# Eleven small stores of the first chunk, issued from ScalarE's queue instead of SyncE's

## The chip, the core and the metric

The kernel runs on one core of a Trainium2 chip. The core has compute engines that work side by side (here VectorE, ScalarE and a little GpSimd are used), a SyncE that does no arithmetic and issues transfers, and 16 DMA engines that move data between the memory of the chip (HBM) and the core's own memory (SBUF, 128 partitions). A transfer is issued on a queue that belongs to the issuing engine; SyncE and ScalarE have one each, GpSimd has one that is filled by software. The metric is the device time of one execution in microseconds; less is better.

## What is computed

The input `logits` has the shape (2, 8, 2112, 2112) in fp32, 285 MB; the output has the same shape. A bias that depends on the distance of row and column is added, then a softmax is taken along the last axis:

```python
pos = np.arange(S)                                   # S = 2112
rel_clipped = np.clip(pos[:, None] - pos[None, :], -16, 16) + 16
logits = logits + rel_bias[:, rel_clipped][None]     # rel_bias: (8, 33)
logits = logits - logits.max(axis=-1, keepdims=True)
exp = np.exp(logits)
return exp / exp.sum(axis=-1, keepdims=True)
```

Every element is read once and written once.

## The kernel before

The 33,792 rows of the input are dealt to the 128 partitions: each holds `ROWS` = 264 rows that lie next to each other in HBM. They are worked through in `N` = 44 chunks of `R` = 6 rows per partition, 128 x 12,672 elements each (6336 KB), in `NBUF` = 4 buffers `X0` to `X3`. `STEP` = 24 rows are one round of all four buffers.

*A chunk's way.* SyncE loads it (`load`, L99). VectorE adds the bias row by row and takes the row's maximum (`add`, L238). ScalarE takes EXP of the row and its sum (`exps`, L247). VectorE then inverts three sums at a time (L255) and multiplies the three rows (L259, `scale`), raising the semaphore `scaled` by one per row. SyncE waits for six scaled rows and stores the chunk (`store`, L104). Ahead of the first chunk VectorE builds a table of the bias, for which ScalarE loads `rel_bias` (L122); GpSimd meanwhile prepares row numbers for its own late stores.

*What sets the order.* Each engine runs its instructions in the order of the code and waits on semaphores that the others raise; nothing is planned by a scheduler. SyncE first issues the loads of chunks 0 to 3 one behind the other (L129). Then it waits for chunk 0 (L285) and stores it in two portions. Rows 2 to 5 go as one transfer of 128 partitions (L286). Rows 0 and 1 go as eleven transfers (`parts`, L274 to L283): the list `AHEAD` says at which partition each begins and how many it takes, 15, 13, 4, 16, 16, 16, 9, 7, 14, 10 and 8, always every fourth partition. Each of the k partitions of such a transfer is given to another DMA engine, the first k of the 16. So one DMA engine gets from 3 to 11 of the 128 pieces of 16,896 bytes, where a transfer of all 128 partitions gives 8 to each. Near the end two other lists, `BEHIND` (SyncE, four transfers of 16) and `LAST` (GpSimd), share out rows 3 to 5 of chunk 41 (L296, L297, L159) in the opposite way.

All twelve transfers of chunk 0 raise the semaphore `main`. GpSimd waits until all twelve have landed (L169) and then raises `st[0]` in their name (L170). In the loop (L288 to L292) SyncE by turns stores the next chunk and, once the store before it has landed (`st[b]`), loads a new chunk into the buffer that has become free. The first reload, of `X0`, thus waits for the eleven small transfers too.

ScalarE's part is one loop of eleven rounds of four chunks (L268 to L270).

## Time and profile before

| | |
|---|---|
| time, median of 3 runs (lowest to highest) | 1331.28 us (1330.13 to 1331.38) |
| time of the profiled execution | 1331.03 us |
| its span, from the first to the last instruction | 1329.3 us |
| HBM read, written | 285.49 MB, 288.31 MB |
| SyncE's longest kind of wait (semaphores, L96) | 1251.0 us in 85 waits |
| loads of a chunk, issue to landing (median of 44) | 44.6 us |
| stores of a chunk, issue to landing (median of 41) | 52.6 us |

The page gives busy times for the span and for 40 equal slices of 33.2 us each; each digit is a busy share in tenths. A row of the timeline has a start, a duration, an engine (with a "q" for its instruction queue, as in SPq, where DMAs are issued), a line, an operation, and in brackets the idle time ahead of it and what ended that. The stretch view counts a packet's bytes and time in the stretch where it starts, so over a few microseconds the rate swings and a share may exceed 1. Issuing a DMA is short; moving its data comes later, when the queue has reached it.

### The profile page before, as it was taken

Reading aid. Unit: us, or ns where it says so; the run is one execution under the profiler, and the core shown is the slowest. Engines: PE = TensorE matmul, PEld = TensorE weight load, DVE = VectorE, ACT = ScalarE, POOL = GpSimd, SP = SyncE. Lnnn points to the kernel's source line nnn. Section 1 sums busy time; section 2 is a strip of 40 time slices with the busy share of each in tenths; the row PEclk is TensorE's granted clock in tenths of the full one; section 3 lists DMA queues with packets and bytes.
Section 4 is the critical chain, followed back from the end, with each engine's and each line's share of the span. In section 5 each row is a group of like instructions: output and inputs, shape, how many; then the busy total and the mean of one; then the engine's idle time right before and its main releaser. Section 6 shows DMA issues by size and latency. Waiting matters only on the chain. (4 is left out here: it accounts for less than half of the span.)

```text
span 1329.3 us, 2545 instructions
## 1 busy us (share of the span) xinstructions
DVE 977.7 (74%) x917; ACT 575.2 (43%) x539; POOL 10.0 (1%) x41
## 2 busy tenths in 40 slices
DVE  7997777677877786677778777677877786677763
ACT  3474433434444443334445433434444443334442
POOL 1000000000000000000000000000000000000100
DMA  9999999999999999999999999999999999999998
GB/s 413 414 387 427 435 435 433 435 433 435 432 436 433 433 433 433 436 435 433 432 436 433 432 435 433 435 435 435 435 432 435 432 433 435 435 435 433 433 434 356
DMA packets 13492, 571.01 MB, mean 430 GB/s; under 512 B 1824, under 2 KB 1840, under 8 KB 1840
## 3 DMA queue, kind: packets, MB, share of 16 engines
q1 hardware_dynamic: 13200, 569.33, 99.4%
q0 software_dynamic: 256, 1.62, 0.3%
q14 instruction: 4, 0.03, 0.0%
q10 hardware_dynamic: 32, 0.02, 0.0%
HBM read 285.49 MB, written 288.31 MB: 432 GB/s over the span
## 5 line engine op out<-in xcount | busy, mean ns | idle before, releaser
L238 DVE CUSTOM_DVE_ANT_0 X<-X,F 128x2112 f32<-128x2112 f32 x264 | 605.2, 2354 | 308.9 <-DVEq L96 308.9
L247 ACT ACTIVATE X<-X,nmax 128x2112 f32<-128x2112 f32 x264 | 541.7, 2052 | 539.3 <-ACTq L96 517.5
L259 DVE TENSOR_SCALAR X<-X,rec 128x2112 f32<-128x2112 f32 x264 | 332.4, 1315 | 13.2
L247 ACT ACT_TABLE_LOAD x11 | 14.1, 1283 | 188.6 <-ACTq L96 188.6
L247 ACT ACTIVATION_READ_ACCUMULATOR X<-X,nmax 128x1 f32 x264 | 49.2, 186 | 0.0
L232 DVE COPY F<-M 128x2135 f32 x11 | 26.1, 2374 | 0.5 <-DVEq L261 0.5
L238 DVE DVE_READ_ACCUMULATOR2_ANT nmax<- 128x1 f32 x264 | 21.7, 82 | 0.0
L255 DVE RECIPROCAL rec<-tot 128x3 f32<-128x3 f32 x88 | 14.9, 170 | 0.0
L159 POOL DMA_INDIRECT out_dram<-X,sel x5 | 4.5, 897 | 1239.3 <-POOLq L96 1238.1
L194 DVE TENSOR_TENSOR F<-F 128x264 f32<-128x264 f32 x1 | 0.4, 433 | 7.1 <-DMA F<-in_rel_bias_dram 7.1
L150 POOL TENSOR_SCALAR_AFFINE_SELECT sel<-sel 128x1 int32<-128x1 int32 x25 | 4.7, 190 | 3.6 <-POOL sel L144 0.2
L224 DVE COPY M<-F 128x1848 f32<-128x1848 f32 x1 | 2.1, 2077 | 0.0
L119 DVE MEMSET F<- 128x264 f32 x1 | 0.3, 278 | 1.1 <-SPq L79 1.1
L144 POOL IOTA sel<- 128x1 int32 x5 | 0.6, 127 | 0.0
L198 DVE TENSOR_REDUCE F<-F 128x33 f32<-128x264 f32 x1 | 0.6, 608 | 0.0
L221 DVE TENSOR_TENSOR M<-F 128x264 f32<-128x264 f32 x1 | 0.4, 441 | 0.0
L213 DVE TENSOR_TENSOR F<-F,rbS 128x264 f32<-128x264 f32 x1 | 0.4, 426 | 0.0
L191 DVE TENSOR_SCALAR F<-F 128x8 f32<-128x8 f32 x4 | 0.4, 165 | 0.0
L226 DVE COPY M<-rbS 128x247 f32<-128x247 f32 x1 | 0.4, 406 | 0.0
L206 DVE STREAM_TRANSPOSE F<-F 128x64 f32<-128x64 f32 x1 | 0.2, 246 | 0.0
L201 DVE STREAM_TRANSPOSE F<-F 128x64 f32<-128x64 f32 x1 | 0.2, 245 | 0.0
L211 DVE TENSOR_SCALAR F<-F,rbS 128x8 f32<-128x8 f32 x1 | 0.2, 231 | 0.0
(18 smaller groups left out, 2.8 us busy)
## 6 DMA issues: line engine op xcount, KB each, us to landing
X<-in_logits_dram SPq DMA_DIRECT2D x44, 6336.0 KB, 44.6
out_dram<-X SPq DMA_DIRECT2D x41, 6336.0 KB, 52.6
out_dram<-X SPq DMA_DIRECT2D x3, 3168.0 KB, 19.1
out_dram<-X SPq DMA_DIRECT2D x1, 4224.0 KB
out_dram<-X SPq DMA_DIRECT2D x4, 396.0 KB, 45.6
out_dram<-X SPq DMA_DIRECT2D x3, 264.0 KB
out_dram<-X SPq DMA_DIRECT2D x1, 247.5 KB
out_dram<-X SPq DMA_DIRECT2D x1, 231.0 KB
```

Of the source, the lines that this page charges most:

```text
L144: step(g.iota(col, pattern=[[0, 1]], base=(p0 * ROWS + row) // unit, channel_multiplier=lap * ROWS // unit))
L150: step(g.affine_select(out=col, in_=col, pattern=[[0, 1]], base=base, channel_multiplier=mul, compare_op=op, fill=float(FAR)))
L159: g.indirect_dma_start(out=blocks, out_offset=bass.IndirectOffsetOnAxis(ap=sel[0:n, w : w + 1], axis=0), in_=bass.AP(tensor=x.tensor, offs ...
L191: then(v.tensor_scalar(out=m, in0=dp, scalar1=0.0, scalar2=None, op0=op))
L194: then(v.tensor_tensor(out=view(F, 0, [[W, H], [1, W]]), in0=view(F, 0, [[W, H], [1, W]]), in1=view(F, SC + 3 * PB, [[1, H], [0, W]]), op= ...
L198: then(v.tensor_reduce(out=F[:, RB : RB + W], in_=view(F, 0, [[1, W], [W, H]]), axis=mybir.AxisListType.X, op=ALU.add))
L224: then(v.tensor_copy(out=view(M, U + W, [[ROWS, PB], [1, ROWS - W]]), in_=view(F, SC + 7 * PB, [[1, PB], [0, ROWS - W]])))
L232: v.tensor_copy(out=F[:, :], in_=M[:, bass.ds(ROWS - STEP - j, FW)]).then_inc(dve, 1)
L238: v.tensor_tensor_reduce(out=x, in0=x, in1=F[:, STEP - 1 - r : STEP - 1 - r + S], scale=-1.0, scalar=BIG, op0=ALU.add, op1=ALU.min, accum_ ...
L247: nc.scalar.activation(out=x, in_=x, func=EXP, scale=-1.0, bias=nmax[:, r : r + 1], accum_out=tot[:, r : r + 1],).then_inc(expd, 1)
L255: v.reciprocal(out=rec[:, r0 : r0 + HALF], in_=tot[:, r0 : r0 + HALF]).then_inc(inv, 1)
L259: v.tensor_scalar_mul(out=x, in0=x, scalar1=rec[:, r : r + 1]).then_inc(scaled, 1)
```

## The change

A new semaphore `half` is added. `parts` gets the issuing engine as a parameter. ScalarE's first round is taken out of the loop and written out; between its first chunk's six EXPs and those of the second, ScalarE waits for `half` and issues the eleven transfers `AHEAD` on its own queue. SyncE raises `half` when three rows of chunk 0 are scaled (the two that are stored are among them), and no longer issues the eleven.

```diff
+        half = nc.alloc_semaphore("half")
...
-        with nc.Fori(0, ROWS // STEP, 1, engines=[ENG.Activation]):
-            for b in range(NBUF):
-                exps(b)
-        def parts(own, x, r0, r1, j, sem):
+        def parts(eng, own, x, r0, r1, j, sem):
             step_p = list(x.ap[0])[0]
             for p, k in own:
-                nc.sync.dma_start(
+                eng.dma_start(
...
+        for b in range(NBUF):
+            exps(b)
+            if b == 0:
+                take(nc.scalar, half, 1)
+                parts(nc.scalar, AHEAD, X[0], A0, A1, 0, main)
+        with nc.Fori(1, ROWS // STEP, 1, engines=[ENG.Activation]):
+            for b in range(NBUF):
+                exps(b)
+
+        nc.sync.wait_ge(scaled, HALF)
+        nc.sync.sem_inc(half, 1)
         take(nc.sync, scaled, R)
         nc.sync.dma_start(out=rows(out, A1, R - A1), in_=X[0][:, A1 * S : R * S]).then_inc(main, 16)
-        parts(AHEAD, X[0], A0, A1, 0, main)
...
-        parts(BEHIND, late, Z0, Z1, (N - 3) * R, st[(N - 3) % NBUF])
+        parts(nc.sync, BEHIND, late, Z0, Z1, (N - 3) * R, st[(N - 3) % NBUF])
```

In the lists of instructions that follow, `X_58` to `X_61` are the buffers X0 to X3, `out_dram` is the output, and a shape is partitions x elements. Line numbers are each kernel's own; L278 of before is L273 of the change, L100 is L101, L104 is L105.

SyncE before, from the last initial load to the first reload:

```order
L100 DMA X_61<-in_logits_dram 128x12672
L119 UNCONDITIONAL_BRANCH
L286 DMA out_dram<-X_58 128x8448
L278 DMA out_dram<-X_58 15x4224
L278 DMA out_dram<-X_58 13x4224
L278 DMA out_dram<-X_58 4x4224
L278 DMA out_dram<-X_58 16x4224 x3
L278 DMA out_dram<-X_58 9x4224
L278 DMA out_dram<-X_58 7x4224
L278 DMA out_dram<-X_58 14x4224
L278 DMA out_dram<-X_58 10x4224
L278 DMA out_dram<-X_58 8x4224
```

SyncE in the change, the same place and on to the first reload:

```order
L101 DMA X_61<-in_logits_dram 128x12672
L120 UNCONDITIONAL_BRANCH
L292 DMA out_dram<-X_58 128x8448
L293 UNCONDITIONAL_BRANCH
L105 ISA
L105 DMA out_dram<-X_59 128x12672
L101 ISA
L101 DMA X_58<-in_logits_dram 128x12672
```

Behind the four-row store the eleven rows are gone; the store of the second chunk is next.

ScalarE in the change, from the table load of its first EXP to the second chunk (before, its one loop has the four rows of EXPs and nothing between them):

```order
L248 ACT_TABLE_LOAD
L248 ACTIVATE X_58,tot<-X_58,nmax 128x2112 x6
L273 DMA out_dram<-X_58 15x4224
L273 DMA out_dram<-X_58 13x4224
L273 DMA out_dram<-X_58 4x4224
L273 DMA out_dram<-X_58 16x4224 x3
L273 DMA out_dram<-X_58 9x4224
L273 DMA out_dram<-X_58 7x4224
L273 DMA out_dram<-X_58 14x4224
L273 DMA out_dram<-X_58 10x4224
L273 DMA out_dram<-X_58 8x4224
L248 ACTIVATE X_59,tot<-X_59,nmax 128x2112 x6
```

The eleven transfers stand between the first chunk's EXPs and the second's. The loop that follows holds no table load any more; the one ahead of the first EXP is the only one.

## Prediction

> **What bounds the kernel now.** I read the page's head first: the busy shares of the engines, the 40 slices, the queues.

> ```profile
> span 1329.3 us, 2545 instructions
> DVE 977.7 (74%) x917; ACT 575.2 (43%) x539; POOL 10.0 (1%) x41
> DMA  9999999999999999999999999999999999999998
> GB/s 413 414 387 427 435 435 433 435 433 435 432 436 433 433 433 433 436 435 433 432 436 433 432 435 433 435 435 435 435 432 435 432 433 435 435 435 433 433 434 356
> q1 hardware_dynamic: 13200, 569.33, 99.4%
> ```

> No compute engine is full, but the 16 DMA engines are busy in every slice, and 99.4% of their time goes to one queue, q1, SyncE's. So the time is the bytes divided by the rate, plus whatever keeps the rate low. The rate sits at 432 to 436 GB/s from the fifth slice on; it is lower in the first four and the last. The change touches the first four, so I cut them at what the queue carries, and set the long middle beside them (columns: stretch, its length, busy time of three engines, clock, DMA share, GB/s).

> ```profile
> 20.00:60.00 40.00, 39.40 (x38) 26.51 (x25) 0.00 (x0) 1.00 0.99 430
> 60.00:75.00 15.00, 15.00 (x14) 9.43 (x9) 0.00 (x0) 1.00 0.95 381
> 75.00:90.00 15.00, 14.70 (x15) 6.59 (x7) 0.00 (x0) 1.00 1.04 380
> 90.00:115.00 25.00, 18.03 (x17) 9.76 (x10) 0.00 (x0) 1.00 0.99 406
> 115.00:160.00 45.00, 34.06 (x31) 23.18 (x22) 0.00 (x0) 1.00 1.00 435
> 160.00:1240.00 1080.00, 796.39 (x733) 472.72 (x444) 0.00 (x0) 1.00 1.00 434
> ```

> The loads before 60 us and everything after 115 us run at full rate. Between 60 and 115 us the engines are as busy as ever (0.95 to 1.04) and move less: packets take longer there, nobody waits for work. What is that worth? The DMA view of each stretch gives bytes and packet time; first the middle, then 60 to 75, 75 to 90 and 90 to 115 us:

> ```profile
> q1 hardware_dynamic: 10399, 468.56, 100.2%
> q1 hardware_dynamic: 228, 5.71, 95.1%
> q1 hardware_dynamic: 285, 5.69, 103.6%
> q1 hardware_dynamic: 229, 10.14, 99.4%
> ```

> In the middle a megabyte costs 1.002 x 1080 / 468.56 = 2.310 us on all 16 engines. At that price 5.71 MB is 13.19 us and took 0.951 x 15 = 14.27, **1.08 us lost**; 5.69 MB is 13.14 and took 15.54, **2.40 lost**; 10.14 MB is 23.42 and took 24.85, **1.43 lost**. Together 4.9 us are all that can be won here.

> Which transfers are these? SyncE's own rows:

> ```profile
> 0.96 1.90 SPq L100 DMA_DIRECT2D X<-in_logits_dram  x4
> 41.05 0.34 SPq L286 DMA_DIRECT2D out_dram<-X  x1
> 41.43 8.34 SPq L278 DMA_DIRECT2D out_dram<-X  x11
> 62.92 0.37 SPq L104 DMA_DIRECT2D out_dram<-X  x1
> 86.34 0.37 SPq L100 DMA_DIRECT2D X<-in_logits_dram  x1
> ```

> One queue is served in order. Four loads of 6336 KB (25.95 MB) take 59.9 us at 2.310, from about 3 us on, so to about 63; the four-row store (4.33 MB, 10.0 us) follows to about 74; then come the eleven small transfers. They hold 2.16 MB, which is 5.0 us at full rate, and the next store mixes in behind them. So 75 to 90 us is the stage of the small transfers, and its 2.40 us are theirs: their partitions are unevenly shared out (3 to 11 pieces for one DMA engine), and engines work side by side on pieces that are not a regular 128-partition pattern. That this pattern is the cause is my reading; that the stage is slow is measured.

> **The change part by part.** *The queue.* The eleven transfers leave SyncE's queue and go to ScalarE's, so they need not wait for the backlog. Does such a transfer pass the loads? One in this trace did:

> ```profile
> F<-in_rel_bias_dram ACTq DMA_DIRECT2D x1, 16.5 KB, 8.1
> ```

> It landed 8.1 us after issue while 60 us of loads stood in SyncE's queue. So the pieces will mix with the load packets: 0.62 us for a piece (16,896 bytes), 1.87 for a load packet (50,688 bytes), both at 2.310, so 2.5 us for a pair. An engine with 11 pieces is through in 27 us, one with 3 in 7. Starting at about 37 us they fit amid the loads, which then end about 5 us later. The bytes are the same, so nothing is gained by being earlier; gained is only what the pieces lose among themselves now. In the loads a piece has on average one neighbour in four that is also a piece, not fifteen.

> What do they cost there? The trace doesn't show strided pieces amid loads. Bounds: the same 2.40 us as now, or nothing. The nearest row is 1240 to 1300 us, where 256 pieces of a second queue and 64 small ones of SyncE mix with loads and stores:

> ```profile
> q1 hardware_dynamic: 704, 24.33, 94.0%
> q0 software_dynamic: 256, 1.62, 6.4%
> ```

> 25.95 MB took 1.004 x 60 = 60.24 us against 59.93 at 2.310: **0.31 us**. I take that and keep 0 to 2.40 for the range. Saved: 2.40 − 0.31 = 2.09.

> *The stage behind, 90 to 115 us.* Its 1.43 us are ordinary stores and loads, run by engines that the small transfers have pushed out of step. They will be out of step after the change too, as the shares of 3 to 11 stay, but will turn from loads to stores that way. No row says which; between 0 and 1.43 I take half, 0.72. The 1.08 us of 60 to 75, where loads turn into stores, I leave: that turn stays.

> *The time at the end.* Do 2.8 us saved at 60 to 115 us reach the end? Every slice shows busy DMA, and the longest wait at the end (the first row, SyncE's) is for a store to land; the compute engines have slack, VectorE 9.03 us in the second row, at the first load that the loop issued:

> ```profile
> SPq L304 <- DMA out_dram<-X: 13.9, 1, 13.9
> 117.36 2.36 DVE L238 CUSTOM_DVE_ANT_0 X<-X,F 128x2112 f32<-128x2112 f32 x1 [9.03 <-DVEq L96]
> ```

> So the whole saving goes through.

> *ScalarE.* It now waits for a signal and issues eleven transfers between its sixth and seventh EXP.

> ```profile
> 33.16 3.77 DVE L259 TENSOR_SCALAR X<-X,rec 128x2112 f32<-128x2112 f32 x3
> 35.08 0.18 ACT L247 ACTIVATION_READ_ACCUMULATOR X<-X,nmax 128x1 f32 x1
> 43.13 0.08 DVE L238 DVE_READ_ACCUMULATOR2_ANT nmax<- 128x1 f32 x1
> 43.34 2.05 ACT L247 ACTIVATE X<-X,nmax 128x2112 f32<-128x2112 f32 x1 [8.07 <-ACTq L96]
> 54.53 0.08 DVE L238 DVE_READ_ACCUMULATOR2_ANT nmax<- 128x1 f32 x1
> 56.70 0.19 ACT L247 ACTIVATION_READ_ACCUMULATOR X<-X,nmax 128x1 f32 x1
> 58.55 0.17 DVE L255 RECIPROCAL rec<-tot 128x3 f32<-128x3 f32 x1
> ...
> L247 ACT ACT_TABLE_LOAD x11 | 14.1, 1283 | 188.6 <-ACTq L96 188.6
> ```

> Three rows are scaled at 33.16 + 3.77 = 36.93; ScalarE stands idle from 35.26 to 43.34. The issues took SyncE 8.34 us, so from 36.9 they end near 45.3: the seventh EXP is 2.0 us late. Behind it five more are queued, at 2.05 us each where VectorE delivers one row in 2.28 ((54.53 − 43.13) / 5), so 0.23 is caught up per row and the twelfth is 0.9 late, ending near 57.8; VectorE wants it at 58.55. Hidden by 0.7 us, and if that cover goes, by the 9.03 us above. SyncE loses 8.34 us of issuing, before a wait that ends at 62.92 for scaled rows of the next chunk: worth nothing. GpSimd, which counts the twelve first stores as landed and lets SyncE reload X0 (86.34 us), does so about 5 us earlier; the queue has the second store ahead of it, so the engines don't see it. The unrolled first round leaves one table load (1.28 us) where there were eleven; ScalarE waits 188.6 us ahead of those, so nothing comes of it.

> The sum: 1331.03 (this execution; its span is 1329.3) − 2.40 + 0.31 − 0.72 = **1328.2 us**. The runs shown have a median of 1331.28, 0.25 us above this execution, so that is 0.23% under them. About 0.2% (2.7 us) is what a measurement of this kernel can tell from no change.

> [...]

> **The rivals.** *No gain (0.32).* The pieces are as dear amid the loads, or the loads beside them suffer: the 2.40 us move to 37 to 65 us and the 1.43 stay. For it: engines still get 3 to 11 pieces. Against it: 0.31 us at the end. Time 1331.0.

> *Slower (0.10).* Each piece makes its engine turn from reading HBM to writing it and back. The turn at 60 to 75 us cost 1.08 us an engine. An engine has 8 pieces on average; at the full price that is 8.6 us, and 1331.03 − 3.12 + 8.6 = 1336.5. It undoes the gain from 0.39 us a piece (3.12 / 8), and is slower by over 0.2% from 0.72 ((3.12 + 2.66) / 8). Against it is the middle, where these

> ```profile
> X<-in_logits_dram SPq DMA_DIRECT2D x36, 6336.0 KB, 44.6
> out_dram<-X SPq DMA_DIRECT2D x36, 6336.0 KB, 52.6
> ```

> make some 72 turns at the base price.

> *More gain (0.10).* Pieces in the loads also stagger the turn at 60 to 75, and all three losses go: 1331.03 − 4.9 = 1326.1.

> *The change does nothing*, as the pieces come late or ScalarE is held at its issues until the loads drain: then its EXPs stop for up to 20 us. SyncE issued all eleven in 8.34 us, 25 us before the first could move, so issuing does not wait for moving. Its time is that of no gain, and its chance is in there.

> **How the numbers follow.** The forecast, 1328.2, gets 0.48, spread by about 1.5 us to both sides; of that 0.40 lies over 0.2% below the median. With more gain (0.10): faster 0.50. No gain and the rest of the forecast: same 0.40. Slower: 0.10. The range runs from 1325.4, just past the full gain, to 1333.0, two microseconds past no gain, which leaves out most of the slower case.

> **What would show it.** Right: small packets on ScalarE's queue (q10) between 37 and 65 us, that stretch near 430 GB/s, 75 to 90 us too, and the first reload issued about 5 us before 86.34. Of the terms: 37 to 65 us shows the 0.31, the 25 us after the first store the 0.72. Wrong: 37 to 65 us near 380 to 400 GB/s (the loss has moved), or a late seventh EXP with VectorE waiting near 58 us. If the rates rise as told and the time doesn't fall, the sum fails at the end of the kernel, where the last of 16 engines decides and not their mean.

## The result, and the profile after

The change is a little slower, by 0.16%: a median of 1333.62 us (1329.82 to 1334.58, 18 runs) against 1331.33 us (1329.93 to 1332.57, 18 runs); the ratio is 1.0016, with a 95% interval from 1.0010 to 1.0022. The forecast was 1328.2 us, the range 1325.4 to 1333.0. Of the 18 runs 17 took 1332.12 us or more; one took 1329.82. The profiled execution took 1332.85 us, its span is 1331.1 us; it stands for most runs, not for all.

The slices of the page, which for the kernel before began with 413 414 387 427:

```profile
GB/s 414 415 425 423 430 436 434 436 431 433 434 434 428 437 433 430 430 433 436 433 433 427 439 434 431 434 431 431 434 439 436 428 430 437 439 436 428 430 431 331
```

The dent of the third slice is gone, as forecast. But the slices behind no longer stand at 432 to 436; they dip to 427 to 431 again and again, and the last is 331 where it was 356. The stretches of the prediction show the same (length, busy time of three engines, clock, DMA share, GB/s):

```profile
37.00:60.00 23.00, 22.70 (x22) 12.34 (x12) 0.00 (x0) 1.00 0.98 412
60.00:75.00 15.00, 15.00 (x13) 9.41 (x9) 0.00 (x0) 1.00 0.98 412
75.00:90.00 15.00, 14.70 (x15) 6.68 (x7) 0.00 (x0) 1.00 1.04 441
90.00:115.00 25.00, 20.08 (x18) 9.58 (x10) 0.00 (x0) 1.00 1.00 410
160.00:1240.00 1080.00, 793.02 (x729) 463.78 (x431) 0.00 (x0) 1.00 1.00 433
```

Then bytes and packet time on each queue, q1 for SyncE's and q10 for ScalarE's: two rows each for 37 to 60, 60 to 75 and 75 to 90 us, then 90 to 115 us and 160 to 1240 us.

```profile
q1 hardware_dynamic: 177, 8.16, 84.2%
q10 hardware_dynamic: 140, 1.30, 13.3%
...
q1 hardware_dynamic: 155, 5.51, 87.0%
q10 hardware_dynamic: 93, 0.68, 10.7%
...
q1 hardware_dynamic: 155, 6.42, 100.9%
q10 hardware_dynamic: 23, 0.19, 2.9%
...
q1 hardware_dynamic: 234, 10.24, 100.0%
...
q1 hardware_dynamic: 10378, 467.65, 100.2%
```

At the old price of 2.310 us per MB the first stretch lost 0.975 x 23 − 9.46 x 2.310 = 0.6 us, the second 0.4, the third 0.3, the fourth 1.35: **2.6 us in all, where 5.0 were lost before** (the prediction's 4.9, and 0.1 from 37 to 60 us). The early part went nearly as forecast. The long middle did not stay as it was: in the same 1080 us and with the same packet time it moved 467.65 MB and not 468.56, and 0.91 MB is **2.1 us**.

So the gain is given back between 160 and 1240 us. Who gives it? The records of single packets don't name their DMA engine, but on each engine the packets follow each other almost without a gap (in these two profiles a record starts, in the median, 4 ns before the one ahead of it on its engine ends). So they can be strung into 16 chains, one for each engine, and a packet can be held against the shortest time of its size (1.87 us for 50,688 bytes). Where two engines end within a few nanoseconds of each other the stringing can swap them, so what a single chain lost is good to about half a microsecond. The next table is worked out in that way. "Spacing" is the time from the first engine that ends a given chunk transfer to the last one, near 124 us and near 1217 us. "Middle" is the time by which packets between 160 and 1240 us were longer than their size needs, per engine on average; only packets over 0.05 us too long are counted. "Last" is how far the last engine ends behind the mean of the 16.

```
kernel     spacing at 124 us   at 1217 us   middle    last
before            6.6 us          7.7 us    0.0 us    3.2 us
change            3.8             7.3       2.0       5.1
```

Before, the engines leave the early stage 6.6 us apart, and 15 of the 16 keep their distances to a tenth of a microsecond through the whole kernel; the sixteenth drifts by 3.7 us, in packets that are each less than 0.05 us too long. In the change they leave it 3.8 us apart, draw nearer still (3.1 us at 319 us), and are then pushed apart in steps. Of 126 packets in the middle that took over 0.05 us too long, about 120 are the eighth and last of a transfer on their engine, just ahead of the turn from a load to a store or back. They hit some engines and spare others: six chains lost from 3 to 5 us, four lost 0.1 us or nothing. The last engine decides the time: early −2.4, middle +2.0, last behind mean 5.1 − 3.2 = +1.9, together +1.5 us, against +1.8 us between the two profiled spans. From the ends alone: their mean came 0.2 us earlier (1324.3 us against 1324.5), and the last one 1.9 us further behind it.

**Theory A** from here on: what matters is how far apart the DMA engines are when they turn. **Its rivals**: theory B, the place of the small stores amid the loads upsets the rest; or the second queue costs by itself.

### The profile page after: what moved, and what is told of

It is laid out like the page before. It is cut to its first block, busy times and chain, and to the rows that moved or that the text cites. A ratio compares the mean times of both kernels' runs of the same rounds, so it can differ in the third digit from the quotient of the medians.

```text
span 1331.1 us, 2535 instructions
## 1 busy us (share of the span) xinstructions
DVE 977.9 (73%) x917; ACT 567.2 (43%) x529; POOL 10.1 (1%) x41
## 3 DMA queue, kind: packets, MB, share of 16 engines
q0 software_dynamic: 256, 1.62, 0.3%
## 5 line engine op out<-in xcount | busy, mean ns | idle before, releaser
L248 ACT ACT_TABLE_LOAD x1 | 1.3, 1283 | 21.4 <-ACTq L97 21.4
## 6 DMA issues: line engine op xcount, KB each, us to landing
X<-in_logits_dram SPq DMA_DIRECT2D x44, 6336.0 KB, 44.7
out_dram<-X SPq DMA_DIRECT2D x41, 6336.0 KB, 52.6
```

What stands on the lines that cost most here:

```text
L248: nc.scalar.activation(out=x, in_=x, func=EXP, scale=-1.0, bias=nmax[:, r : r + 1], accum_out=tot[:, r : r + 1],).then_inc(expd, 1)
```

## The experiments

Times are medians of 4 to 11 runs, ratios are against the kernel before on the same chip (1330.9 to 1331.7 us there); the last kernel was run once. Spacing, middle and last are read from one profiled execution of each kernel, whose time may differ from the median by up to 2 us.

**The eleven transfers amid the loads, but on SyncE's queue.**

```diff
-        for n in range(NBUF):
+        for n in range(NBUF - 1):
             load(n * R, n)
...
+        nc.sync.wait_ge(scaled, HALF)
+        parts(AHEAD, X[0], A0, A1, 0, main)
+        load((NBUF - 1) * R, NBUF - 1)
         take(nc.sync, scaled, R)
         nc.sync.dma_start(out=rows(out, A1, R - A1), in_=X[0][:, A1 * S : R * S]).then_inc(main, 16)
-        parts(AHEAD, X[0], A0, A1, 0, main)
```

> The eleven transfers stay on SyncE's queue but stand between the third and the fourth initial load, so they move amid the loads (about 48 to 55 us) in order, one behind the other, with no second queue. Theory A (spacing): what costs the change its gain is that ScalarE's queue deals the pieces out over 40 us, so the 16 DMA engines leave the early stage only 3.8 us apart instead of 6.6, then get in each other's way where they turn between loads and stores; in one queue they leave 5 to 7 us apart wherever the pieces stand. It expects 160 to 1240 us at 2.310 us per MB (as before) and a time within 0.1% of before or up to 2 us below it. Theory B (place): small stores amid loads upset the rest, on whichever queue. It expects the middle above 2.313 us per MB and a time of 1333 to 1334 us, like the change.

Measured: **1327.96 us** (1327.18 to 1328.88), ratio 0.9975 (0.9965 to 0.9985), the best of all kernels here. SyncE's rows and three stretches of it:

```profile
0.96 1.34 SPq L100 DMA_DIRECT2D X<-in_logits_dram  x3
36.79 8.29 SPq L278 DMA_DIRECT2D out_dram<-X  x11
45.12 0.45 SPq L100 DMA_DIRECT2D X<-in_logits_dram  x1
```

```profile
37.00:60.00 23.00, 22.70 (x22) 12.89 (x12) 0.00 (x0) 1.00 0.98 399
90.00:115.00 25.00, 19.00 (x18) 9.60 (x10) 0.00 (x0) 1.00 1.01 438
160.00:1240.00 1080.00, 796.33 (x733) 470.59 (x441) 0.00 (x0) 1.00 1.00 434
```

The pieces still lose something where they run (399 GB/s), but the stage from 90 to 115 us, which lost 1.4 us before and in the change, loses nothing (438 GB/s), and neither does the middle. Spacing 7.6 us, held but for one engine that drifts; middle 0.0 us. The place amid the loads is good; B falls. The gain is larger than A expected (up to 2 us): it is 3.3.

**No small transfers at all.** Chunks 0 and 41 are stored whole; `choose`, `pieces` and GpSimd's part fall away.

```diff
-        take(nc.sync, scaled, R)
-        nc.sync.dma_start(out=rows(out, A1, R - A1), in_=X[0][:, A1 * S : R * S]).then_inc(main, 16)
-        parts(AHEAD, X[0], A0, A1, 0, main)
+        store(0, 0)
...
+        store((N - 3) * R, (N - 3) % NBUF)
...
```

> No small transfers at all: chunk 0 and chunk 41 are stored as one 128-partition transfer each, so every DMA engine gets the same packets all along. Theory A: the engines stay within 1 to 2 us of each other, turn together, and lose time at the turns until they have drifted apart: 160 to 1240 us costs more than in the change (2.314 us per MB), at least 2 us in all, and the time is 1334 us or more. Theory B: with no small stores there is nothing to upset the rest: the middle is at 2.310 and the time 1331 or less, as the 2.4 us of the pieces' own stage are saved.

Measured: 1332.58 us (1330.45 to 1333.80), ratio 1.0011 (1.0002 to 1.0020). From 37 to 115 us it loses 1.2 us, less than any other kernel here, and nearly all of it from 60 to 75 us, where loads turn into stores:

```profile
60.00:75.00 15.00, 15.00 (x13) 9.71 (x9) 0.00 (x0) 1.00 0.99 399
75.00:90.00 15.00, 14.70 (x15) 6.58 (x7) 0.00 (x0) 1.00 1.00 433
90.00:115.00 25.00, 21.60 (x20) 10.84 (x12) 0.00 (x0) 1.00 1.02 438
160.00:1240.00 1080.00, 793.04 (x729) 470.62 (x441) 0.00 (x0) 1.00 1.00 433
```

And yet the time is above before's. Spacing 2.2 us near 124 us, growing to 8.0; middle 1.5 us; ten engines end within 0.5 us of each other, the last six 1.7 to 7.5 us behind those. This fits A: some of the engines that turned close together here lost time, until they were apart. (The late store of chunk 41 was changed as well, so the time compares more than the spacing; the middle lies ahead of that store.) Its sizes were less than A expected (a middle of 1.5 and not 2 us, 1332.58 and not 1334). B's 1331 or less is not met.

**The change with pieces of three rows.** `A0, A1 = 0, 3` in place of `0, 2`.

> The change with pieces of three rows (25,344 bytes) in place of two, so that the shares of 3 to 11 pieces put the engines half as far apart again; the four-row store becomes one of three rows. The late transfers are left as they are, so the end is out of balance by about 1 us more on the engines with most pieces. Theory A: the spacing after the early stage grows from 3.8 to 5 or 6 us, and 160 to 1240 us falls from 2.314 us per MB to 2.311 or less. Theory B: more small stores amid the loads, so the middle and the early stages are as slow as in the change or slower.

Measured: 1328.70 us (1327.97 to 1329.07), ratio 0.9980 (0.9971 to 0.9989). Spacing 5.1 us, middle 0.0, last 2.3 us behind the mean. With half as many bytes again amid the loads the early stretches from 37 to 115 us lose more (3.5 us for 2.6), and the kernel is 4.9 us faster than the change. As A expected.

**The change, issued one chunk later.** `if b == 1:` in place of `if b == 0:`.

> The change with ScalarE issuing the eleven behind the second chunk's EXPs (near 58 us) and not behind the first's (near 37): the second queue stays, but the pieces move amid the stores of chunks 0 and 1, not the loads. Theory A: a second queue deals the pieces out slowly there too, so the engines end 3 to 5 us apart and the middle costs 2.312 us per MB or more; time 1332 to 1335. Theory B (place amid the loads): the middle is at 2.310 and the time is that of before. A third theory, that the second queue costs by itself at each change of queue, expects 60 to 115 us to lose more than the 4.9 us of before.

Measured: 1344.43 us (1342.57 to 1345.62), ratio 1.0101 (1.0086 to 1.0117). No theory had this size. Its stretches, and SyncE's row for the first reload:

```profile
60.00:75.00 15.00, 15.00 (x14) 9.36 (x9) 0.00 (x0) 1.00 0.95 395
75.00:90.00 15.00, 14.70 (x15) 6.68 (x7) 0.00 (x0) 1.00 1.02 403
90.00:115.00 25.00, 17.90 (x17) 9.63 (x10) 0.00 (x0) 1.00 0.86 334
```

```profile
98.19 0.36 SPq L101 DMA_DIRECT2D X<-in_logits_dram  x1
```

The reload of X0 was issued at 98.19 us; before it was at 86.34. It waits for all twelve stores of chunk 0, and the packets show why they were late. This is one DMA engine with eleven pieces, in the change itself (start in us from the start of the span, queue, bytes):

```
42.4  q10  16896   piece
43.0  q1   50688   load
44.9  q10      4   semaphore
44.9  q1   50688   load
46.9  q10  16896   piece
47.5  q1   50688   load
49.4  q10      4   semaphore
49.4  q1       4   semaphore of the load
49.4  q10  16896   piece
50.1  q1   50688   load
51.9  q10      4   semaphore
51.9  q1   50688   load
53.8  q10  16896   piece
54.4  q1   50688   load
56.3  q10      4   semaphore
```

The two queues took turns strictly on this engine: a load packet, a piece, a load packet, the four bytes that raise the piece's semaphore, a load packet. A piece and its semaphore took two turns, so a piece came every 4.4 us and not every 2.5. (Once, at 49.4 us, the load's own semaphore takes SyncE's turn, and two pieces stand 2.5 us apart.) In the change the pieces run from 42 to 80 us, here from 59 to 97 us. GpSimd passes the signal on when the last has landed, SyncE issues nothing meanwhile, and the DMA engines run dry (share 0.86). They meet again there, 1.1 us apart at 124 us, and lose 1.9 us in the middle. The theory that the second queue costs by itself expected 60 to 115 us to lose more than 4.9 us. More was lost there, but not by dearer packets: at 2.310 us per MB the packets were 4.2 us too long, before 4.9, and for 3.9 us the engines stood idle. After 1240 us they run dry once more (a share of 0.83 from 1300 to 1320 us, before 0.98); why was not followed further.

**Equal shares at the best place.** The kernel without small transfers, but rows 0 and 1 of chunk 0 go as one 128-partition transfer between the third and the fourth load.

```diff
+        nc.sync.wait_ge(scaled, HALF)
+        nc.sync.dma_start(out=rows(out, 0, A1), in_=X[0][:, 0 : A1 * S]).then_inc(main, 16)
+        load((NBUF - 1) * R, NBUF - 1)
...
```

> As in the kernel without small transfers, but rows 0 and 1 of chunk 0 are stored as one 128-partition transfer between the third and the fourth initial load: the place that was best, with equal shares for all DMA engines. Theory A (spacing): the place alone brings little; the engines stay within 2 us of each other after the loads, some lose 3 to 6 us at the turns between 120 and 1240 us (2.312 us per MB or more there), and the time is 1330.5 to 1333. Rival (the place is what counts): the middle is at 2.310 and the time 1329 or less, as with the eleven transfers at this place.

Measured: 1331.92 us (1330.95 to 1333.48), ratio 1.0009 (1.0000 to 1.0018). Spacing 3.1 us, middle 1.8, last 5.9 us behind the mean. The place without the uneven shares is worth next to nothing (ratio 1.0009, where the kernel without small transfers has 1.0011); with them it was worth 3.3 us.

**The change with steeper shares.** Same queue, place, size of pieces and bytes; twelve transfers in place of eleven.

```diff
-    RUNS = [(15, 13, 4), (16, 16), (16, 9, 7), (14, 10, 8)]
+    RUNS = [(15, 12, 5), (16, 11, 5), (16, 9, 7), (12, 10, 10)]
```

> The change (ScalarE's queue, behind the first chunk's EXPs) with the same bytes in the same size of pieces, dealt more unevenly: 12 transfers that give a DMA engine from 2 to 12 pieces in place of 3 to 11. The late transfers stay, so the end is out of balance by one piece (0.6 us) more. Theory A: the spacing after the early stage grows from 3.8 to about 5 us and 160 to 1240 us goes from 2.314 us per MB to 2.311 or less; time 1329 to 1331.5. Rival (three-row pieces helped because the store behind them is shorter, not by spacing): the middle stays at 2.313 or above, the time at 1333 to 1334.5.

Measured: **1328.66 us** (1328.54 to 1328.87), ratio 0.9981 (0.9972 to 0.9990). Its middle, to be held against the change's 467.65 MB:

```profile
q1 hardware_dynamic: 10396, 468.56, 100.2%
```

Spacing 4.9 us, middle 0.1, last 2.3 us behind the mean. A share of 2 to 12 pieces in place of 3 to 11 makes the kernel 5.0 us faster: by the two profiles the middle is worth 1.9 of it, the last engine 2.8. This is the nearest pair of kernels in the study, and the second queue is in both. The time is even a little below what A expected.

**The best place with three rows.** `A0, A1 = 0, 3` on SyncE's queue.

> SyncE's queue, between the third and the fourth load, with pieces of three rows. Theory A: the spacing grows from about 7 to 10 us, but the middle is at 2.310 already and can't get better; the pieces are half as long again, so their own stage loses about 0.7 us more, and the end is out of balance by about 1 us more: time 1328.5 to 1330. Rival (more spacing is always better): below 1327.5.

Measured: 1329.89 us (1328.77 to 1331.12), ratio 0.9993 (0.9984 to 1.0002). Spacing 8.7 us, middle 0.0; the stretches from 37 to 115 us lose 2.7 us and not 1.8, and the last engine is 4.3 us behind the mean and not 3.5. So more spacing won nothing more in the middle here, and the longer pieces cost at both ends.

**The best place, chunk 41 stored whole.** Nothing undoes the uneven shares at the end.

> The eleven transfers on SyncE's queue between the third and the fourth load, and chunk 41 stored as one transfer, so nothing at the end undoes the uneven shares. Theory A with its second half (the time is that of the DMA engine that ends last, not of their mean): the middle stays at 2.310, the engines end about 7 us apart, those with 11 pieces last, 1.9 us of pieces behind the mean share; time 1327 to 1330. If the mean decided, the time would be that of the kernel with the late transfers, 1328, or below, as their 0.3 us of loss are saved.

Measured: 1329.88 us (1329.60 to 1331.23), ratio 0.9988 (0.9979 to 0.9997). The engines end on average 0.4 us earlier than with the late transfers (1320.7 us from the start of the span against 1321.2), but the last one is 5.1 us behind that mean and not 3.5, and the time is 1.9 us longer. The last engine decided here, not the mean.

**The change once more.**

> The change itself once more, for a second profile: theory A expects the spacing after the early stage to be 3 to 4.5 us again, 160 to 1240 us to cost 2.312 to 2.316 us per MB, and the DMA engine that ends last to be 4 us or more behind the mean.

Measured: 1334.09 us, one run. Spacing 4.2 us, middle 1.5, last 6.1 us behind the mean; the middle's rate is again 433 GB/s where before has 434:

```profile
160.00:1240.00 1080.00, 794.51 (x730) 464.31 (x432) 0.00 (x0) 1.00 1.00 433
```

All of it beside each other, by the same reading of the packets:

```
kernel                             time us   spacing at 124 us   middle   last
before                             1331.3           6.6           0.0      3.2
change                             1333.6           3.8           2.0      5.1
change, once more                  1334.1           4.2           1.5      6.1
no small transfers                 1332.6           2.2           1.5      5.8
equal shares amid the loads        1331.9           3.1           1.8      5.9
change, steeper shares             1328.7           4.9           0.1      2.3
change, three rows                 1328.7           5.1           0.0      2.3
SyncE's queue amid the loads       1328.0           7.6           0.0      3.5
the same, three rows               1329.9           8.7           0.0      4.3
the same, chunk 41 whole           1329.9           7.6           0.0      5.1
change, one chunk later            1344.4           1.1           1.9      5.4
```

Where the engines left the early stage 4.9 us apart or more, in six of these profiles, the middle cost 0.1 us or nothing; in the five with 4.2 us and less it cost 1.5 to 2.0 us on average, and more on single engines, up to 5 or 6. This is the spread of all sixteen, and not the distance of any two: in the kernel before, three engines turn within 0.1 us of each other from 125 to 1232 us and lose nothing.

## Why the prediction was wrong

*What bounds the kernel.* Right: the DMA engines, in every kernel here (their packets took 100.2% of the time from 160 to 1240 us), and the losses lay between 60 and 115 us.

*The stage of the small transfers.* Right in kind and nearly in size. The stretches from 37 to 90 us, which lost 3.5 us before (1.08 and 2.40), were to lose 1.39 (1.08 and 0.31) and lost 1.2. That the total fits is partly luck: from 37 to 60 us, amid the loads, the loss was 0.6, and the rate of 412 GB/s there lies between the near 430 that was to show the forecast right and the 380 to 400 that was to show it wrong; from 60 to 75 us it was 0.4 and not 1.08. The stage behind was to fall from 1.43 to 0.71 and stayed at 1.35. The whole early gain is 2.3 to 2.4 us; forecast were 2.8.

*The pace of the pieces.* Wrong: "through in 27 us" reckoned one load packet to a piece. Semaphores took turns too (4.4 us from piece to piece), and the pieces began at 42 and not at 37 us; they ended at 80 and not at 64. In the change this hurt nothing directly, since the reload still came earlier than before (82.23 us and not 86.34; forecast was about 81). Issued one chunk later, the pieces held the reload back to 98.19 us, and the engines ran dry (a share of 0.86 from 90 to 115 us).

```profile
82.23 0.36 SPq L101 DMA_DIRECT2D X<-in_logits_dram  x1
```

*ScalarE.* Right within half a microsecond:

```profile
36.88 8.71 ACTq L273 DMA_DIRECT2D out_dram<-X  x11
45.73 2.06 ACT L248 ACTIVATE X<-X,nmax 128x2112 f32<-128x2112 f32 x1 [10.66 <-ACTq L97]
57.89 0.19 ACT L248 ACTIVATION_READ_ACCUMULATOR X<-X,nmax 128x1 f32 x1
58.36 0.17 DVE L256 RECIPROCAL rec<-tot 128x3 f32<-128x3 f32 x1
```

The seventh EXP began at 45.73 (forecast near 45.3), and the twelfth's sum was read by 58.08, 0.3 us ahead of VectorE's next step. Nothing waited.

*"They will be out of step after the change too, as the shares of 3 to 11 stay", and "so the whole saving goes through".* **This is the step that failed.** By the sum, eight pieces (11 less 3) of 0.62 us are 5.0 us of spacing in either queue. But the losses come on top: before, engines with many and with few pieces lost about as much between 20 and 120 us (about 3 to 6 and 5 us by their packets). In the change the engines with 3 and 4 pieces, which are first at every turn, lost 4.0 and 2.9 us and those with 11 mostly 1.6 to 2.0, so 3.8 us of spacing were left, where the prediction held the spacing to be unchanged. Behind that stand the two terms that the sum put at nothing: the middle, which cost 2.0 us, and the last engine, 1.9 us further behind the mean. They outweigh the 2.4 us won early. That the losses close the gap is read from the packets of these two profiles; it was not tried by itself. What the smaller spacing does was tried: steeper shares alone turned +2.3 us against before into −2.25 (1328.66 against 1330.91). I took the busy DMA of the middle for a fixed price per byte; in these kernels that price went with the spacing set up in the first 115 us. The prediction named the last engine as the place where the sum could fail, and gave that no term.

*The rivals.* None was the right one. The slower one priced turns from load to store at the pieces themselves, with the gain undone from 0.39 us each. There the turns were cheap: 37 to 60 us, with 1.30 MB of pieces, lost 0.6 us in all. The dear turns were those of the large transfers, over the thousand microseconds that follow (2.0 us per engine). No gain, 1331.0, came nearer than my sum, but not for its reason: the early rate did rise, from 380 to 441 GB/s between 75 and 90 us, and the same queue with steeper shares is 2.25 us below before.

*What stays open.* Why packets at the turns took longer where the spread was small (2.0 us per engine in the change), and on some engines only: the records show where and how long, not what is waited for. That the spread itself decides, and not something else that goes with the shares, is what all eleven traces agree with; it was always set by the shares, never by other means. And spread does not explain the stretch from 90 to 115 us: it is free with 7.6 us made amid the loads and with the 2.2 us of equal shares, and not with 6.6 us made behind the loads.

## What to carry to other kernels

Here 16 DMA engines were busy throughout, and the time was that of the engine that ended last (3.2 us behind the mean before, 5.1 in the change). The price of a byte went with how far apart the engines ran: 0.91 MB less in the same 1080 us when they left the early stage 3.8 us apart and not 6.6. In such a kernel, compare bytes moved in the same long stretch, before and after, and the spread of the engines' ends, not only the stage that was edited. If small uneven transfers set up that spacing, keep them on the queue of the large ones, or try steeper shares when they move: amid the loads on the same queue they were worth 3.3 us here, and steeper shares on the second queue 5.0 us. The small transfers on a second queue were not served at once but by turns with large packets, their semaphores included (eleven pieces took 37 us), so put nothing urgent behind the landing of many of them.
